# Block 1's activations fetched after the third modulation tile and built alternately with block 0's, in a four-branch decoder layer

## The chip, the cores and the metric

The kernel runs on one core of a Trainium2 chip. The metric is the device time of one execution in microseconds (us), the median of several runs; less is better. PE is the matrix engine, ACT the scalar engine, DVE the vector engine, POOL the GpSimd engine, and SP the queue from which most transfers are issued.

## The reference

One layer, 2048 tokens of width 1024. The conditioning vector gives a shift, a scale and a gate; the normalized input goes through one wide projection whose columns feed three branches (a gated linear recurrence, HGRN2 with 4 heads, a Mamba-2 scan with 16 heads); their outputs go through one output projection and a last normalization.

```python
cond = silu(c)
shift, scale, gate = split(cond @ w_ada + b_ada, 3)
h = rmsnorm(x, norm_w) * (1 + scale) + shift
u = h @ w_in                     # 1024 -> 5648 columns
a_x, a_g, hg_q, hg_f, hg_i, hg_g, ssd_z, ssd_xbc, ssd_dt = split(u)
ya = rg_lru(causal_conv(a_x)) * silu(a_g)
yb = rmsnorm(hgrn2(silu(hg_q), hg_f, hg_i)) * silu(hg_g)
yc = grouped_rmsnorm((ssd(xbc, dt) + d * xs) * silu(ssd_z))
out = rmsnorm(x + gate * (concat(ya, yb, yc) @ w_out), final_norm_w)
```

## The kernel before

The 2048 tokens are four blocks of 512 (tb 0 to 3), taken in two halves of two. Each block's normalized input is eight feature tiles of 128 x 512 (k = 0 to 7), stored as a rounded value and the rest (`ht`, two planes). Every projection is three matmuls per feature tile: high by high, high by low, low by high (`proj_mm`, L339). The weights are split the same way: ACT writes the rounded value, POOL or DVE the rest (`split`, L141 and L142).

**The order of instructions.** PE's order is the order of the code. On the other engines a scheduler chooses the order when the program is built; `after(ins, name)` adds an order without a wait on the chip. Each engine then works its list strictly in order. Loads of 256 KB go out from SP; each waits until the load eight places before it has landed.

**The start** is written out in the string `PROG`, one word per step, played by the loop over `PROG.split()`. `Xn` loads the eight feature tiles of block n (2 MB), `Dj` loads modulation tile j (four loads), `w0`/`w1` the two halves of the first head's three weights (three loads each), and `W0`/`W1` split them. `Sn` squares block n's tiles on ACT (`xsq`) and adds them on DVE, `Qn` sums over features on PE (`ps_ss`) and takes the root and reciprocal, and `Rn` spreads the result over the partitions on PE (`ps_rb`) and copies it out on ACT (`rb`). `Aj` multiplies modulation tile j on PE (`psm`, 8 instructions, 16 matmuls in the trace) and copies it out on ACT (`macc`); `Cj` turns it into a column on PE (`psm` again, 2 instructions) and DVE writes shift and scale for feature tile j (`gsc`). `Hnk` builds feature tile k of block n: DVE scales (`h_pre`, the `xt` row), ACT rounds (`ht`, L330), DVE writes the rest (`ht` again). `Mnk` multiplies it with all three weights: 9 matmuls, three each into `ps_f`, `ps_q` and `ps_g`. `Un` is n filler matmuls (`warm`), `B` starts the loading of later weights, `K` loads constants. `E` orders the first evacuations behind the last `H` step.

After the start come the two heads' value projections (`ps_v`) and the HGRN2 heads. `weave` lays the pieces of a generator such as `hgrn` between the pieces of the projections that run meanwhile, by weights: a branch's piece comes when its share of the total weight is reached. `hgrn` begins with small matmuls `ps_sA` that need `hg_q` and `hg_k`, and ends with `ps_o`, one PSUM bank from the pool `ps_oy`, which has a single bank.

For the second half, `norm_stats` squares and sums rows on ACT while the Mamba part runs (`xst`); `norm_gen` (L883), called in step i = 2 of the recurrence part for block 2 and at the head of the second half for block 3, takes root and reciprocal of `xst` and goes straight on to `ps_rb`:

```python
    def norm_gen(xs, st):
        rb = norm_rows(rsqrt_cols(st))
        yield
```

At the end the output projection runs in units of one token tile and one branch; `fetch` (L912) loads the branch's result for the next unit, rounds it on ACT and writes the rest (`yy`) on POOL.

Of the kernel before, what the change touches and what calls it, by code (L numbers as in the profile page):

```python
# [8 lines left out]
F32 = mybir.dt.float32  # L9
F32R = mybir.dt.float32r  # L10
BF16 = mybir.dt.bfloat16
U8 = mybir.dt.uint8
# [6 lines left out]
P = 128  # L19
# [12 lines left out]
for _name, _w in (("norm_w", 8), ("b_shift", 8), ("b_scale", 8), ("c", 8),  # L32
# [5 lines left out]
NCOL = _n  # L38
NTMP = 32
NW = 8  # L40
PROG = ("X0 D0 w0 D1 D2 S0 U8 A0 Q0 U1 C0 D3 R0 W0 A1 U1 C1 H00 D4 A2 M00 C2 H01 w1 W1 D5 A3 M01 C3 H02 D6 A4 M02 C4 H03 X1 "
        "A5 M03 C5 H04 D7 A6 M04 C6 H05 S1 M05 H06 Q1 A7 R1 M06 C7 H10 H07 B K M10 H11 M11 H12 M07 H13 M12 H14 M13 "
        "H15 M14 H16 M15 H17 E M16 M17")
LW = 4
BW = (4, 1)
L0 = 0.01
# [3 lines left out]
def trunk(ctx, tc, x, x_t, w_mod, w_gate, w_in, w_out, wa, wx, cols, rows, ident_in,  # L50
# [271 lines left out]
        act(rb, ps, AF.Copy)  # L322
        return rb

    def h_pre(xs, rb, k):
        stt(xs[k], xs[k], gsc[:, 1, k:k + 1], rb, MUL, MUL)

    def h_tile(xs, k, dep=None):
        ht = hp.tile([P, 2, TB], F32R, tag="h", name="ht")
        d_ = S.activation(ht[:, 0], xs[k], AF.Identity, bias=gsc[:, 0, k:k + 1])  # L330
        after(d_, dep)
        stt(ht[:, 1], xs[k], gsc[:, 0, k:k + 1], ht[:, 0], ADD, SUB)
        return ht, d_.ins.name

    PASSES = ((0, 0), (0, 1), (1, 0))

# [124 lines left out]
    def consts(dep):  # L461
        mf = tmp("mf", (P, 6, 32), bufs=1)
        for d_, s_ in ((mf, masks_in), (tri, tri_in)):
            after(nc.sync.dma_start(d_, s_), dep)
        for gi, wsrc in ((0, wa), (1, wx)):
            for hh in range(2):
                after(nc.sync.dma_start(wab[hh * 64:(hh + 1) * 64, gi, :, hh * 64:(hh + 1) * 64],
                                        wsrc.rearrange("(t two) i j -> two i t j", two=2)[hh]), dep)
        after(nc.sync.dma_start(rowp, rows[0:1, 0:32].to_broadcast([P, 32])), dep)
        V.tensor_copy(maskd, mf[:, 0])  # L470
        V.tensor_copy(masks, mf[:, 1:6])

    def early():
        e4 = tmp("e4", (P, 4), bufs=1)
        p4 = tmp("p4", (P, 4), bufs=1)
        cs4 = tmp("cs4", (P, 4), bufs=1)
        tt(V, e4, cc("hlb", 0, 4), cc("hlb", 0, 4), MAX)
        tt(V, e4, cc("hlb", 0, 4), e4, SUB)
        sact(e4, e4, AF.Exp)
        V.reciprocal(p4, e4)  # L480
        tt(V, p4, e4, p4, MUL)
        V.tensor_copy(cs4, p4)
        tt(V, omlb[:, 0], cs4, p4, SUB)
        V.tensor_scalar(omlb[:, 1], omlb[:, 0], -1.0, 1.0, op0=MUL, op1=ADD)
        V.tensor_scalar(e4, cc("lam", 0, 4), -1.0, None, op0=MUL)
        softplus(cpos[:, 1], e4, 4, sact)
        V.tensor_scalar(cpos[:, 1], cpos[:, 1], 8.0, None, op0=MUL)
        V.tensor_scalar(cpos[:, 0], cpos[:, 1], -1.0, None, op0=MUL)
        V.tensor_scalar(dhalf, cc("sd", 0, 8), 0.5, None, op0=MUL)

    early()
# [61 lines left out]
    def hgrn(h, tbs, fq, vs, acc, first):  # L553
# [85 lines left out]
        st = hst[h]  # L639
        for n, tb in enumerate(tbs):  # L640
            v, gs, f, pkv = vs[tb], GS[n], Fs[n], pkvs[n]
            po = bank(ps_oy, "oy", "ps_o", (P, 4, P))
            for c in range(4):
                ci = 4 * tb + c
                PE.matmul(po[:, c], v[:, c], ssb[:, 4 * n + c], start=True, stop=ci == 0)  # L645
                if ci == 0:
                    V.tensor_copy(st, pkv[:, c])
                else:
                    PE.matmul(po[:, c], st, Qs[n][:, c * P:(c + 1) * P], start=False, stop=True)
                    if ci < 4 * NTB - 1:  # L650
                        stt(st, st, Tm[n][:, c:c + 1], pkv[:, c], MUL, ADD)
                if c < 3:
                    yield
            pof = po.rearrange("p c n -> p (c n)")
            if not first:
                act(f, pof, AF.Square)
                tt(G, acc[tb], acc[tb], f, ADD)
            else:
                act(acc[tb], pof, AF.Square)
            tt(V, gs, pof, gs, MUL)  # L660
            put_y(tb, 4 + h, gs)
            yield
# [218 lines left out]
        yield  # L881

    def norm_gen(xs, st):  # L883
        rb = norm_rows(rsqrt_cols(st))
        yield
        for k in range(KT):
            h_pre(xs, rb, k)
            if k % 4 == 3:
                yield
# [2 lines left out]
        for w_ in itertools.islice(g, n):  # L892
            yield w_

    def gap():
        yield

    def h_build(tb, xs, hts, dep):
        for k in range(KT):
# [31 lines left out]
    for half in range(2):  # L931
# [4 lines left out]
        for p in range(2):  # L936
# [26 lines left out]
            if half == 0 and p == 0:  # L963
# [3 lines left out]
                             bank(ps_mm, "mm", "ps_g") if tb == 0 else bank(ps_oy, "oy", "ps_g")]  # L967
                        for tb in tbs}
                xsb, sts, u_, dn, hn = {}, {}, None, None, None
                sqs = [[hp.tile([P, 2, TB], F32, tag="h", name="xsq") for _ in range(4)] for _ in tbs]  # L970
                x0s = [wp.tile([P, 2, TB], F32, tag="w", name="xt") for _ in range(4)]
                for op_ in PROG.split():
                    o_, ar = op_[0], [int(c) for c in op_[1:] if c.isdigit()]
                    if o_ == "D":
                        mod_dma(ar[0])
                    elif o_ == "A":
                        mod_mm(ar[0])
                    elif o_ == "C":
                        mod_col(ar[0])
                    elif o_ == "X":  # L980
                        xsb[ar[0]] = load_x(ar[0], x0s if ar[0] == 0 else None)
                    elif o_ == "S":
                        sts[ar[0]], dn = norm_sum(xsb[ar[0]], sqs[ar[0]])
                    elif o_ == "Q":
                        sts[ar[0]] = norm_cols(sts[ar[0]])
                    elif o_ == "R":
                        sts[ar[0]] = norm_rows(sts[ar[0]])
                    elif o_ == "E":
                        evac[0] = hn
                    elif o_ == "H":  # L990
                        h_pre(xsb[ar[0]], sts[ar[0]], ar[1])
                        HTS[ar[0]][ar[1]], hn = h_tile(xsb[ar[0]], ar[1])
                    elif o_ == "w":
                        for b_ in WBL[0:3]:
                            if ar[0] == 0:
                                b_.alloc()
                            b_.fetch(ar[0])
                    elif o_ == "W":
                        for b_ in WBL[0:3]:
                            b_.parts(ar[0], *((dn, V) if ar[0] == 0 else (hn, G)))  # L1000
                    elif o_ == "U":
                        pu = bank(ps_ms, "ms", "warm", (P, 4, P))
                        for _ in range(ar[0]):
                            PE.matmul(pu, ones, ones.unsqueeze(1).to_broadcast([P, 4, P]), start=True, stop=True)
                    elif o_ == "K":
                        consts(u_)
                    elif o_ == "B":
                        blocks.dep = u_
                        blocks.pump()
                    elif o_ == "M":  # L1010
                        tb, k = ar
                        for w_, ps in zip((wf, wq, wg), accs[tb]):
                            u = u_ = proj_mm(ps, w_, HTS[tb][k], k)
# [20 lines left out]
                    run(ps_, pend)  # L1034
            if half == 1 or p == 1:
                first = []
            pend = [(hgrn(h, tbs, {tb: fq[h, tb] for tb in tbs}, {tb: vs[tb][0] for tb in tbs}, acc, h == 0), HGW)]
            h += 1
            ps_ = first
            for f in (pf, pq_, pg):  # L1040
# [1 line left out]
                for tb in tbs:  # L1042
                    ps_ += f(w, h, tb)
            run(ps_, pend)
            pend = [(hgrn(h, tbs, {tb: fq[h, tb] for tb in tbs}, {tb: vs[tb][1] for tb in tbs}, acc, False), HGW)]
        if half == 0:
            act(aneg, rowp[:, 16:32], AF.Exp)
            V.tensor_scalar(aneg, aneg, -1.0, None, op0=MUL)
        dt_ = [(ssd_dt(tb, dtr[tb], dts), 1) for tb in tbs]
        st_ = [(stats(acc[tb], 0, tb), 2) for tb in tbs]  # L1050
        pend = dt_ + pend + st_
# [31 lines left out]
        for i in range(4):  # L1083
# [5 lines left out]

            def pgl(tb):  # L1090
                return p_proj(wg, HTS[tb], "ps_lg", lambda ps: gs.__setitem__(tb, lru_g(ps)))
            if i == 2 and half == 0:
                xs_ = load_x(2)
                pend += [(norm_gen(xs_, xst[0]), 3)]
# [122 lines left out]

    for u in range(len(units)):
        if u + 1 < len(units):
            fetch(u + 1)  # L1220
        pcs = unit(u) if u + 1 < len(units) else last_unit(u)
        if u == 0:
            weave(pcs, pend)
            for k in (12, 13, 14, 15):
                OBlock(k, hp, "h", h_use[id(HTS[3][2 * (k - 12) + 1])])
            OBlock(0, op, "wo")
        elif u == 1:
            weave(pcs, [(gate_rows(), 1)])
            OBlock(1)
            OBlock(2)  # L1230
            OBlock(3)
        else:
            for f in pcs:
                f()
        if units[u][1] == FAMS[-1] and u + 1 < len(units):
            for t in groups[units[u][0]]:
                finish(t)
# [60 lines left out]
```

## Time and profile before

| | |
|---|---|
| median of 3 runs | 1697.59 us (1697.58 to 1697.99) |
| the profiled execution | 1699.3 us, of which span 1697.5 us |
| PE busy | 1653.0 us, 97% of the span |
| PE weight loads | 1349.2 us, 79% |
| DVE / ACT / POOL busy | 971.5 / 748.6 / 757.3 us (57%, 44%, 45%) |
| mean granted PE clock | 0.992 |
| DMA | 150.60 MB, mean 89 GB/s; 333 GB/s in the first fortieth of the span |

The span is one execution from its first to its last instruction. Busy shares are averages over stages; where PE is busy all the time, only work taken from PE or waits of PE shorten the run. A busy PE at a lower clock is still counted as busy. "Granted clock" is the share of full speed (2.4 GHz) that PE had; 0.50 is 1.2 GHz.

### The profile page before, as it was taken

To read this page: it belongs to the slowest core of one execution; us is meant where nothing else is said; L and a number is where in the kernel's file an instruction comes from. 1 tells how busy PE (TensorE), PEld (TensorE's weight loads), DVE (VectorE), ACT (ScalarE), POOL (GpSimd) and SP (SyncE) were. 2 spreads that over 40 slices of the span, in tenths; PEclk is the share of its full clock that TensorE was granted. 3 is DMA by queue.
4 is the path that set the end of the run, shared out by engine and by line. 5 is a ranking of instruction groups with operands and counts; after the bars stand their busy time and mean duration, and the time that the engine had idled before them with its cause. 6 is when DMAs were issued, how large, how long until landed. Compare 5 with 4: busy or idle time off the path is not lost.

```text
span 1697.5 us, 29336 instructions
## 1 busy us (share of the span) xinstructions
PE 1653.0 (97%) x11452; PEld 1349.2 (79%) x11452; DVE 971.5 (57%) x1726; ACT 748.6 (44%) x1640; POOL 757.3 (45%) x630
## 2 busy tenths in 40 slices
PE   8799999999999999899999999999999999999998
PEld 4688877888887877788887788888877777888886
DVE  5654766557645746646756555655568646444443
ACT  4422323366556656632322456554757623222221
POOL 1233344355635764345334346545756543222223
PEclk9899999999999999999999999999999999999999
DMA  9412010032425342231110032323334544333231
GB/s 333 116 26 63 27 39 26 26 113 82 116 71 155 88 125 76 62 89 45 29 55 27 27 100 75 94 56 106 88 103 133 171 120 150 97 96 99 89 93 61
DMA packets 177691, 150.60 MB, mean 89 GB/s; under 512 B 14545, under 2 KB 137937, under 8 KB 177553
## 3 DMA queue, kind: packets, MB, share of 16 engines
q1 hardware_dynamic: 141216, 123.82, 25.1%
q10 hardware_dynamic: 33936, 17.04, 3.4%
q0 software_dynamic: 2400, 7.87, 1.3%
q8 instruction: 90, 1.47, 0.4%
q14 instruction: 49, 0.39, 0.1%
HBM read 123.40 MB, written 25.30 MB: 88 GB/s over the span
## 4 chain that ended last, share of the span: by engine, by line
PE 85%; DVE 4%; DMA 3%; ACT 3%; issue 3%; POOL 2%; SPq 0%; POOLq 0%; ACTq 0%; DVEq 0%
PE po L1138 19%; PE ps_x L339 10%; PE ps_z L339 9%; PE ps_v L345 6%; PE ps_f L339 5%; PE ps_g L339 5%; PE ps_bc L339 5%; PE ps_q L339 4%; PE ps_lg L339 4%; PE ps_lx L339 4%; PE ps_y L792 2%; PE ps_bx L768 2%; PE ps_y L797 1%; PE ps_sA L565 1%; PE ps_o L645 1%
## 5 line engine op out<-in xcount | busy, mean ns | idle before, releaser
L1138 PE MATMUL po<-wo,yy 128*128 128x512 f32 x1512 | 353.3, 395 | 2.5 <-POOL yy L69 1.6
L1138 PEld LDWEIGHTS po<-wo,yy 128*128 128x128 f32 x1512 | 283.8, 188 | 71.5 <-POOL yy L69 2.4
L142 POOL TENSOR_TENSOR w<-raw,w 128x512 fp32r<-128x512 f32 x156 | 219.6, 1426 | 266.9 <-ACT w L141 223.4
L72 DVE SCALAR_TENSOR_TENSOR cacc<-craw,col,cacc 128x512 f32<-128x512 f32 x192 | 203.8, 1062 | 47.6 <-ACT cacc L66 36.3
L339 PE MATMUL ps_z<-ht,w 128*128 128x512 f32 x768 | 190.2, 399 | 0.8 <-ACT halo L66 0.8
L339 PE MATMUL ps_x<-ht,w 128*128 128x512 f32 x768 | 190.4, 400 | 0.0
L339 PEld LDWEIGHTS ps_z<-ht,w 128*128 128x128 f32 x768 | 141.9, 188 | 34.7 <-issue 2.1
L339 PEld LDWEIGHTS ps_x<-ht,w 128*128 128x128 f32 x768 | 141.1, 189 | 28.6
L72 DVE SCALAR_TENSOR_TENSOR o<-po,rstd,o 128x512 f32<-128x512 f32 x64 | 47.2, 749 | 119.4 <-PE po L1138 98.8
L69 POOL TENSOR_TENSOR yy<-yr,yy 128x512 fp32r<-128x512 f32 x61 | 78.7, 1310 | 80.7 <-ACT yy L66 73.4
L69 POOL TENSOR_TENSOR hg_k<-hg_k,hg_t 128x256 f32<-128x256 f32 x80 | 60.2, 770 | 120.6 <-PE ps_sA L565 61.3
L141 ACT ACTIVATE w<-raw 128x512 fp32r<-128x512 f32 x158 | 92.3, 627 | 42.0 <-issue 22.0
L339 PE MATMUL ps_f<-ht,w 128*128 128x512 f32 x384 | 99.5, 406 | 5.4 <-DVE ht L72 5.4
L339 PE MATMUL ps_bc<-ht,w 128*128 128x512 f32 x384 | 101.0, 406 | 0.0
L345 PE MATMUL ps_v<-vw,ht 128*128 128x264 f32 x768 | 98.8, 289 | 0.0
L339 PE MATMUL ps_q<-ht,w 128*128 128x512 f32 x384 | 98.7, 403 | 0.0
L339 PE MATMUL ps_lx<-ht,w 128*128 128x512 f32 x384 | 97.7, 408 | 0.0
L345 PEld LDWEIGHTS ps_v<-vw,ht 128*128 128x128 f32 x768 | 95.7, 191 | 1.2 <-DVE l_gs L69 0.2
L69 POOL TENSOR_TENSOR s_ce<-s_ce,cacc 128x512 f32<-128x512 f32 x64 | 93.5, 1481 | 1.5 <-ACT s_ce L66 1.5
L339 PE MATMUL ps_lg<-ht,w 128*128 128x512 f32 x384 | 93.2, 397 | 0.0
L339 PE MATMUL ps_g<-ht,w 128*128 128x512 f32 x336 | 92.0, 408 | 0.0
L339 PEld LDWEIGHTS ps_f<-ht,w 128*128 128x128 f32 x384 | 71.2, 191 | 23.4 <-DVE ht L72 5.7
(260 smaller groups left out, 2853.1 us busy)
## 6 DMA issues: line engine op xcount, KB each, us to landing
raw<-in_w_in SPq DMA_DIRECT2D x176, 256.0 KB, 3.2
s_cb<-crd SPq DMA_DIRECT2D x64, 256.0 KB, 3.8
yr<-yscr SPq DMA_DIRECT2D x64, 256.0 KB, 3.2
xr<-in_x SPq DMA_DIRECT2D x48, 256.0 KB, 3.4
xt<-in_x_t SPq DMA_DIRECT2D x32, 256.0 KB, 4.7
wta<-in_w_mod SPq DMA_DIRECT2D x32, 256.0 KB, 5.9
yscr<-cacc ACTq DMA_DIRECT2D x32, 256.0 KB, 2.7
rawo<-in_w_out SPq DMA_DIRECT2D x32, 256.0 KB, 3.9
```

Source lines behind the costliest of these rows:

```text
L69: e.tensor_tensor(o, a, b, op=op)
L72: V.scalar_tensor_tensor(o, a, s, b, op0=op0, op1=op1)
L141: after(S.activation(hi, raw, AF.Copy), None if eng is V else dep)
L142: after(eng.tensor_tensor(lo, raw, hi, op=SUB), dep if eng is V else None)
L339: d_ = PE.matmul(ps, b.hl[wl][:, k, :], ht[:, hl, :], start=(k == 0 and n == 0), stop=(k == KT - 1 and n == 2))
L345: d_ = PE.matmul(ps[:, 0:264], ht[:, hl, c * P:(c + 1) * P], b.vw[k // 4][wl][:, k % 4, :], start=(k == 0 and n == 0), stop=(k == KT - 1 a ...
L565: PE.matmul(out(n, c, r), Ks[n][:, o:o + 32], mv[n][..., o + sh:o + sh + 32], start=True, stop=True)
L645: PE.matmul(po[:, c], v[:, c], ssb[:, 4 * n + c], start=True, stop=ci == 0)
L768: PE.matmul(pkv[:, c].rearrange("p h n -> p (h n)"), bt[:, c], xw[:, c].rearrange("p h n -> p (h n)"), start=True, stop=True)
L792: PE.matmul(py[64 * hh:64 * hh + 64, c], xdt[:, c, hh], Ms[hh][:, c], start=True, stop=sv[tb][c] is None)
L797: PE.matmul(py[64 * hh:64 * hh + 64, c], sv[tb][c][:, 64 * hh:64 * hh + 64], Cs[hh][:, c * P:(c + 1) * P], start=False, stop=True)
L1138: PE.matmul(pss[t, n], yys[u, t][yl][:, k4, :], wts[4 * fam + k4][wl][n], start=(k4 == 0 and i == 0), stop=(k4 == 3 and i == 2))
```

## The change

`PROG` is rewritten. `X1` stands after `D2` (it stood after `H03`), and the steps of block 1 alternate with those of block 0, so that the eight `M` steps of block 1 no longer follow the block 0 steps. Two more filler matmuls (`U2`) stand ahead of `M03`. `h_pre` gets an order: behind the second-last feature tile's low part on DVE. The staging tiles change pools: block 0's x lies in the pool of the feature tiles, the squares of both blocks share four tiles in the weight pool. The row constants load from ACT's queue at the start. The root of `xst` for both blocks is taken in step i = 1. Every `hgrn` gets a `gap(2)` ahead of it, the second `ps_o` takes a bank of the pool `ps_sc`, and the rest `yy` for units 4 and 5 is written by DVE.

```diff
-PROG = ("X0 D0 w0 D1 D2 S0 U8 A0 Q0 U1 C0 D3 R0 W0 A1 U1 C1 H00 D4 A2 M00 C2 H01 w1 W1 D5 A3 M01 C3 H02 D6 A4 M02 C4 H03 X1 "
...
+PROG = ("X0 D0 w0 D1 D2 X1 S0 U8 A0 Q0 U1 C0 D3 R0 W0 A1 U1 C1 H00 H01 A2 M00 C2 w1 H02 M01 S1 M02 D4 A3 Q1 C3 R1 H03 "
...
-    def h_pre(xs, rb, k):
-        stt(xs[k], xs[k], gsc[:, 1, k:k + 1], rb, MUL, MUL)
+    def h_pre(xs, rb, k, dep=None):
+        after(V.scalar_tensor_tensor(xs[k], xs[k], gsc[:, 1, k:k + 1], rb, op0=MUL, op1=MUL), dep)
...
-        after(nc.sync.dma_start(rowp, rows[0:1, 0:32].to_broadcast([P, 32])), dep)
...
     def early():
+        nc.scalar.dma_start(rowp, rows[0:1, 0:32].to_broadcast([P, 32]))
...
+        sact(aneg, rowp[:, 16:32], AF.Exp)
+        V.tensor_scalar(aneg, aneg, -1.0, None, op0=MUL)
...
-            po = bank(ps_oy, "oy", "ps_o", (P, 4, P))
+            pool, tag = ((ps_oy, "oy"), (ps_sc, "sc"))[n]
+            po = bank(pool, tag, "ps_o", (P, 4, P))
...
     def norm_gen(xs, st):
-        rb = norm_rows(rsqrt_cols(st))
+        rb = norm_rows(st)
...
-    def gap():
-        yield
+    def gap(w=1):
+        yield w
...
-                sqs = [[hp.tile([P, 2, TB], F32, tag="h", name="xsq") for _ in range(4)] for _ in tbs]
-                x0s = [wp.tile([P, 2, TB], F32, tag="w", name="xt") for _ in range(4)]
+                x0s = [hp.tile([P, 2, TB], F32, tag="h", name="xt") for _ in range(4)]
+                sqs = [wp.tile([P, 2, TB], F32, tag="w", name="xsq") for _ in range(4)]
+                los = [None, None]
...
-                        h_pre(xsb[ar[0]], sts[ar[0]], ar[1])
-                        HTS[ar[0]][ar[1]], hn = h_tile(xsb[ar[0]], ar[1])
+                        h_pre(xsb[ar[0]], sts[ar[0]], ar[1], los[-2])
+                        HTS[ar[0]][ar[1]], hn, ln = h_tile(xsb[ar[0]], ar[1])
+                        los.append(ln)
...
-            pend = [(hgrn(h, tbs, {tb: fq[h, tb] for tb in tbs}, {tb: vs[tb][0] for tb in tbs}, acc, h == 0), HGW)]
+            pend = [(gap(2), 2), (hgrn(h, tbs, {tb: fq[h, tb] for tb in tbs}, {tb: vs[tb][0] for tb in tbs}, acc, h == 0), HGW)]
...
+            if i == 1 and half == 0:
+                xst = {n: rsqrt_cols(st) for n, st in xst.items()}
...
-            fetch(u + 1)
+            fetch(u + 1, V if u + 1 in (4, 5) else G)
```

The order on PE in the start, from step `C2` on. `ps_f`, `ps_q` and `ps_g` with three matmuls each are one `M` step; `psm` x2 is a `C` step and `psm` x8 an `A` step. Before:

```order
L450 MATMUL psm<-ones,macc 128x1 x2
L441 MATMUL psm<-wta,condz 32x256 x8
L339 MATMUL ps_f<-ht,w 128x512 x3
L339 MATMUL ps_q<-ht,w 128x512 x3
L339 MATMUL ps_g<-ht,wt 128x512 x3
```

And now, from `M02` on, which directly follows `M01`:

```order
L339 MATMUL ps_f<-ht,w 128x512 x3
L339 MATMUL ps_q<-ht,w 128x512 x3
L339 MATMUL ps_g<-ht,wt 128x512 x3
L441 MATMUL psm<-wta,condz 32x256 x8
L311 MATMUL ps_ss<-ones,xsq 128x1 x4
L450 MATMUL psm<-ones,macc 128x1 x2
L320 MATMUL ps_rb<-ident,xsc 128x128 x4
L1009 MATMUL warm<-ones 128x512 x2
```

Before, each step of block 0 has its `C`, `A` and `M` in turn, and block 1's sum (`ps_ss`) and spreading (`ps_rb`) stand after `M06`. Now `M02` is followed by `A3`, and the sum and the spreading stand ahead of `M03`, with two fillers.

The order on ACT around the second modulation tile's copy (`macc`). Before:

```order
L66 ACTIVATE rb<-ps_rb 128x512
L141 ACTIVATE wt<-raw 128x512
L330 ACTIVATE ht<-xt,gsc 128x512
L66 ACTIVATE macc<-psm 128x256
L330 ACTIVATE ht<-xt,gsc 128x512
```

And now:

```order
L66 ACTIVATE rb<-ps_rb 128x512
L141 ACTIVATE wt<-raw 128x512
L66 ACTIVATE xsq<-xt 128x512
L330 ACTIVATE ht<-xt,gsc 128x512
L66 ACTIVATE xsq<-xt 128x512
L66 ACTIVATE macc<-psm 128x256
L66 ACTIVATE xsq<-xt 128x512 x4
```

Two squares of block 1 now stand ahead of the second `macc`; each needs its tile of block 1's x from memory.

The order on ACT where the roots of `xst` are taken. Before, for block 3, at the head of the second half:

```order
L152 ACTIVATE l_i<-ps_i,col 128x512
L152 ACT_TABLE_LOAD
L152 ACTIVATE xst<-xst,epsc 128x4
L141 ACTIVATE w<-raw 128x512 x2
L66 ACTIVATE rb<-ps_rb 128x512
```

And now, for both blocks, in the recurrence part's first step:

```order
L152 ACTIVATE l_gs<-ps_lg 128x512
L152 ACT_TABLE_LOAD
L152 ACTIVATE xst<-xst,epsc 128x4 x2
L66 ACTIVATE s_z<-cacc 128x512
L520 DMA yscr_100<-cacc 128x4x128
L152 ACT_TABLE_LOAD
L152 ACTIVATE l_r<-ps_r,col 128x512
```

The root for block 3 stood just ahead of the copy `rb` that needs it; now both roots stand between two steps of the recurrence, with a table load on each side.

## Rows read from the trace of the kernel before

**Rows 1.** PE's waits over the span: total us, times, longest.

```profile
PE ps_rb L320 <- DVE xst L285: 7.3, 2, 5.5
PE ps_f L339 <- DVE ht L72: 5.4, 1, 5.4
PE ps_ss L311 <- DVE xsq L305: 3.9, 1, 3.9
PE psm L450 <- ACT macc L66: 2.9, 1, 2.9
...
PE ps_o L645 <- DVE hg_g L69: 1.9, 2, 1.1
...
PE po L1138 <- POOL yy L69: 1.6, 2, 0.9
```

**Rows 2.** Windows: length, busy PE, PEld, DVE, ACT, POOL (count), clock, DMA.

```profile
50.00:55.00 5.00, 3.81 (x25) 2.55 (x26) 1.41 (x5) 0.31 (x2) 0.00 (x0) 0.50 0.63 157
...
65.00:70.00 5.00, 5.00 (x12) 3.91 (x13) 4.84 (x7) 4.17 (x7) 2.58 (x2) 0.51 0.03 10
...
85.00:90.00 5.00, 3.18 (x77) 2.48 (x76) 4.73 (x8) 3.73 (x8) 2.96 (x3) 1.00 0.00 0
```

**Rows 3.** Timeline of PE in the start: start us, us, what [idle before].

```profile
14.65 1.05 PE L311 MATMUL ps_ss<-ones,xsq 128*128 128x1 f32 x8
15.57 1.10 PE L1004 MATMUL warm<-ones 128*128 128x512 f32 x2
16.51 0.50 PE L450 MATMUL psm<-ones,macc 128*128 128x1 f32 x4
16.87 1.14 PE L320 MATMUL ps_rb<-ident,xsc 128*128 128x128 f32 x8
...
38.80 0.96 PE L339 MATMUL ps_f<-ht,w 128*128 128x512 f32 x3
...
40.99 0.50 PE L450 MATMUL psm<-ones,macc 128*128 128x1 f32 x4
41.42 1.07 PE L441 MATMUL psm<-wta,condz 128*32 128x256 f32 x16
...
85.10 0.86 PE L339 MATMUL ps_g<-ht,wt 128*128 128x512 f32 x3
...
88.36 0.65 PE L565 MATMUL ps_sA<-hg_q,hg_k 128*32 128x64 f32 x32 [1.82 <-POOL hg_q L69]
88.95 6.07 PE L345 MATMUL ps_v<-vw,ht 128*128 128x264 f32 x48
```

**Rows 4.** The chain that ended last, first 130 us: start us, us, what.

```profile
13.06 5.69 DMA wta<-in_w_mod
...
18.77 5.86 DMA wta<-in_w_mod
```

**Rows 5.** Timeline of ACT, in the start and in the recurrence part.

```profile
42.65 0.38 ACT L66 ACTIVATE macc<-psm 128x256 f32<-128x256 f32 x1 [2.72 <-PE psm L441]
42.93 0.71 ACT L330 ACTIVATE ht<-xt,gsc 128x512 fp32r<-128x512 f32 x1
43.54 4.26 ACT L66 ACTIVATE xsq<-xt 128x512 f32<-128x512 f32 x8
...
607.99 1.28 ACT L152 ACT_TABLE_LOAD   x1
```

**Rows 6.** Timeline of DVE in the start.

```profile
46.91 0.75 DVE L72 SCALAR_TENSOR_TENSOR xt<-xt,gsc,rb 128x512 f32<-128x512 f32 x1
```

**Rows 7.** Timeline of POOL in the start.

```profile
67.42 3.43 POOL L142 TENSOR_TENSOR vw<-raw,vw 128x512 fp32r<-128x512 f32 x2 [4.56 <-DVE ht L72]
```

**Rows 8.** Timeline of PE where the second half's blocks are normalized.

```profile
647.65 1.16 PE L320 MATMUL ps_rb<-ident,xst 128*128 128x128 f32 x8 [1.79 <-DVE xst L285]
...
693.01 2.08 PE L320 MATMUL ps_rb<-ident,xst 128*128 128x128 f32 x8 [5.51 <-DVE xst L285]
694.74 5.47 PE L345 MATMUL ps_v<-vw,ht 128*128 128x264 f32 x31
```

More of the change, by code (lines that the diff above doesn't have):

```diff
@@ L40 @@
 NW = 8
-PROG = ("X0 D0 w0 D1 D2 S0 U8 A0 Q0 U1 C0 D3 R0 W0 A1 U1 C1 H00 D4 A2 M00 C2 H01 w1 W1 D5 A3 M01 C3 H02 D6 A4 M02 C4 H03 X1 "
-        "A5 M03 C5 H04 D7 A6 M04 C6 H05 S1 M05 H06 Q1 A7 R1 M06 C7 H10 H07 B K M10 H11 M11 H12 M07 H13 M12 H14 M13 "
-        "H15 M14 H16 M15 H17 E M16 M17")
+PROG = ("X0 D0 w0 D1 D2 X1 S0 U8 A0 Q0 U1 C0 D3 R0 W0 A1 U1 C1 H00 H01 A2 M00 C2 w1 H02 M01 S1 M02 D4 A3 Q1 C3 R1 H03 "
+        "H10 U2 W1 M03 D5 A4 M10 H11 C4 M11 H12 H04 M12 H13 M13 D6 A5 M04 H14 C5 H05 M14 D7 A6 M05 H15 C6 H06 M15 A7 M06 H16 C7 "
+        "H07 B K M16 H17 E M07 M17")
 LW = 4
@@ L331, in h_tile @@
         after(d_, dep)
-        stt(ht[:, 1], xs[k], gsc[:, 0, k:k + 1], ht[:, 0], ADD, SUB)
-        return ht, d_.ins.name
+        e_ = V.scalar_tensor_tensor(ht[:, 1], xs[k], gsc[:, 0, k:k + 1], ht[:, 0], op0=ADD, op1=SUB)
+        return ht, d_.ins.name, e_.ins.name
     PASSES = ((0, 0), (0, 1), (1, 0))
@@ L982, in trunk @@
                     elif o_ == "S":
-                        sts[ar[0]], dn = norm_sum(xsb[ar[0]], sqs[ar[0]])
+                        sts[ar[0]], dn = norm_sum(xsb[ar[0]], sqs)
                     elif o_ == "Q":
@@ L1044, in trunk @@
             run(ps_, pend)
[L1045 to L1048, printed above, removed]
+            pend = [(gap(2), 2), (hgrn(h, tbs, {tb: fq[h, tb] for tb in tbs}, {tb: vs[tb][1] for tb in tbs}, acc, False), HGW)]
         dt_ = [(ssd_dt(tb, dtr[tb], dts), 1) for tb in tbs]
```

## The prediction

> **What bounds the kernel now.** I read the page first: PE is busy 97% of the span, every other engine under 60%, so only PE's waits and PE's low clock are to be had. I then listed PE's waits [rows 1]. The reader is to see that few places hold nearly all the idle time: the spreading of the row norms in the middle (`ps_rb`, 7.3 us), three waits in the start (5.4 + 3.9 + 2.9 us), and small ones of 1 to 2 us. Next I asked for the granted clock in short windows [rows 2]: it is 0.50 and 0.51 in the two stretches behind the start's 3.9 and 5.4 us waits, and 1.00 in the stretch that holds the 1.82 us wait of [rows 3]. A long wait is thus paid twice: about 5 us at half clock is another 2.5 us of work, while a wait below 2 us costs itself alone. Last come the timelines of PE, ACT and DVE for the prices of single steps [rows 3, 5, 6].
>
> **The start, before.** The last `M` step ends at 85.10 + 0.86 = 85.96 us [rows 3]. Its waits have one cause: block 1's x is loaded late, its squares are summed late, and block 1's eight `M` steps, all at the end, wait for DVE.
>
> **The start, changed: when PE can go on.** Loads share one stream. The 18th load landed at 13.06 + 5.69 = 18.75 and the 26th at 18.77 + 5.86 = 24.63 [rows 4], so 0.735 us each. Block 1's x now takes places 24 to 31. Its first tile lands at 24.63 - 2 x 0.735 = 23.2. On ACT, two squares now stand ahead of the second `macc`, so this copy, which PE needs for `C1`, is held: 23.2 + 0.53 (square, 4.26 / 8) + 0.71 (`ht`) + 0.53 + 0.38 (`macc`) = 25.3 us [rows 5]. Before, ACT had nothing to wait for there. This is a new wait: behind it on PE stand `C1`, `A2` and everything else. PE has finished `A1` and a filler by about 21, so it idles some 4 us; by [rows 2] I charge 2.5 us of low clock behind it.
>
> The Trainium skill ("TensorE: Matmul & The Clock Gate", Part 1: The HAM clock gate) says that the array is throttled by default and that only recent activity releases it. The two slow stretches of [rows 2] agree.
>
> From 25.3 PE has this work, by start-to-start times where two rows stand next to each other, durations elsewhere [rows 3]: 16 `M` at 40.99 - 38.80 = 2.19 (35.0), 6 `A` at 1.07 (6.4), 7 `C` at 41.42 - 40.99 = 0.43 (3.0), the sum `ps_ss` 15.57 - 14.65 = 0.92, two fillers at 16.51 - 15.57 = 0.94 (1.9) and `ps_rb` 1.14. Together 48.4. Is PE kept fed? `M02` is not: behind `C2` its tile needs two of block 1's adds, its own scaling, ACT's rounding and DVE's rest, five steps of about 0.75 [rows 5, 6], 3.75 in all, while PE has only `M01`, 2.19: it waits 1.6. After that the fillers and `A4` give DVE its lead: a tile costs DVE 2 x 0.75 = 1.5, an `M` costs PE 2.19, so PE is the slower. Only `M07`, one step behind `C7`, may wait again: 0.5. The later modulation tiles need buffers that `M` and `A` steps release, but tile 7 is used about 15 us after that and is covered. Sum: 25.3 + 48.4 + 2.5 + 1.6 + 0.5 = 78.3, a gain of 7.7. Durations overlap a little and some `M` steps follow each other directly, so I take 8.1, bounds 3 (two more waits of the size of `M02`'s with one more slow stretch) and 12 (no slow stretch, no wait of `M02`).
>
> **Behind the start.** `ps_sA` waited 1.82 us for `hg_q`, which came 88.36 - 85.96 = 2.4 us after the last `M`. With the gap, 24 matmuls of `ps_v` at 6.07 / 48 = 0.126 us (3.0 us) stand ahead [rows 3]. But block 0's last `M` now ends only one step before block 1's, so its four evacuations (about 0.5 each) stand ahead of block 1's on ACT: 2.4 + 2.0 against 3.0 leaves 1.4 of wait. Gain 0.4; bounds 0 and 1.8.
>
> **The roots.** In [rows 8] PE waited 1.79 and 5.51 us for the reciprocal of `xst`. Behind the second wait `ps_rb` took 2.08 instead of 1.16, and 31 `ps_v` took 5.47 instead of 31 x 0.126 = 3.9. That is 1.79 + 5.51 + 0.92 + 1.57 = 9.8. The sums `xst` are complete well before the recurrence part, so early roots leave nothing to wait for. What is late next is the copy `rb` and block 3's tiles; [rows 1] has a single wait for `ht`, the start's, so there is room. In the new place ACT pays two table loads of 1.28 [rows 5] and two short roots, some 3 us, between two recurrence steps; PE runs projections meanwhile whose banks are free. If that cover were gone it would cost those 3 us. I take 9.5, bounds 5 and 9.8.
>
> **The small edits.** A second bank for `ps_o` ends its 1.9 us [rows 1]; the gap shifts the first step of every head by about two projection pieces and squeezes the following ones, which may give or cost some tenths at each head: I take 2.0 for both, bounds 0 and 4. Of the 1.6 us for `yy` the larger wait, 0.9, is before a unit whose `yy` DVE now writes; the other unit keeps POOL: 0.9, bounds -0.5 (DVE works its list in order, and a late load would block its evacuations) and 1.6. The constants on ACT's queue, the order hint and the exchanged pools cost nothing of their own: ACT waits for its first input anyway, the hint shapes the DVE order already counted, and the pools set only when buffers come free. If they were exposed, under 1 us.
>
> **Sum.** 8.1 + 0.4 + 9.5 + 2.0 + 0.9 = 20.9. The profiled execution, 1699.3 us with a span of 1697.5, would go to 1678.4; the median of the runs, 1697.6, stands 1.7 below the profiled one, and goes to 1676.7.
>
> **The rivals.**
> *The start gives nothing.* Every step of the start now hangs on in-order lists. ACT splits the value weights only behind the last `macc`, and POOL writes four rests at 3.43 / 2 = 1.7 us beside DVE [rows 7]: 6.9 us, against three `M` steps and a `C` before `ps_v`, 7.0. A little lateness makes PE wait there. For it: [rows 1] shows that such waits did decide the start. Against it: the weights' loads need no late buffer. Then the 8.5 us go and 1685 is left.
> *More than forecast.* No slow stretch, `M02` fed, `ps_sA` and the heads' waits gone: the upper bounds 12 + 1.8 + 9.8 + 4 + 1.6 = 29, time 1668.5.
> *Slower: PE stays at 1.2 GHz through the alternating steps.* The place is the stretch from `C1` on, whose matmuls wait briefly for tiles again and again. An `M` then costs about 2.2 more; all 16 cost 35, less the 2.5 already charged: 32.5 - 20.9 gives 1709. From about ten slow `M` steps on the change loses. For it: the new 4 us wait. Against it: in [rows 3] the same `C`, `A`, `M` alternation ran at 2.19, full speed. The rule of the skill cited above is what would bring this about.
> *The change does not do what it says:* the early x moves the start's waits to the modulation tiles behind it, whose loads come eight places later, and in the roots' place PE waits for `rb`. The time stays near 1697. Against it: eight places are 8 x 0.735 = 5.9 us, less than the start's waits together.
>
> **How the numbers follow.** Forecast 0.64, own range 1671 to 1682; nothing from the start 0.15; more 0.11; slower 0.07; no effect 0.03. The range 1668 to 1687 takes in the second and third case and leaves out 0.10. What differs by over 0.2%, 3.4 us, can be told from no change: faster 0.64 + 0.15 + 0.11 = 0.90, same 0.03, slower 0.07.
>
> **What would show it.** In the changed profile PE waits near 21 to 25 us for ACT's `macc`, the clock is low for about 5 us behind it, then PE is nearly gapless and the last `M` ends near 78. The two waits of `ps_rb` for `xst` are gone and the clock around the second stays at 1.00. The waits of `ps_o` for `hg_g` are gone, that of `ps_sA` is 1 to 2 us. The prediction is wrong if the last `M` ends after 83 or before 74, if `ps_v` waits for `vw`, or if PE waits for `rb` or `ht` where it waited for `xst`.

## The result, and the profile after

The changed kernel takes 1678.88 us (median of four runs, 1676.8 to 1679.21) beside 1697.79 us for the kernel before on the same chip, a ratio of 0.9879 (95% interval 0.9859 to 0.9899): 20.5 us less, between 17.1 and 23.9. The two medians are 18.9 us apart; the ratio is formed over all runs, and of the four before, one took 1702.84, the others 1697.58 to 1697.99. The prediction said 1676.7, with 1668 to 1687 as its range. The profiled execution has a span of 1676.9 us against 1697.5, 20.6 less. PE's busy time went from 1653.0 to 1648.6 us, 98% of the span: 4.4 us of the gain are busy time (slow stretches that went, less two more fillers), the rest is idle time of PE.

PE's waits in the changed kernel, where [rows 1] stood (total us, times, longest):

```profile
PE psm L450 <- ACT macc L66: 2.3, 1, 2.3
PE ps_f L339 <- DVE ht L332: 2.2, 4, 1.0
PE ps_f L339 <- ACT ht L330: 1.6, 3, 0.9
```

`ps_rb` and `ps_o` wait for neither `xst` nor `hg_g` any more. In the start the wait for `macc` is a new one, that of `C1`; the 2.9 us of [rows 1] were `C3`'s and are gone. There are also a number of small waits for `ht`. The timeline of PE there (start us, us, what, [idle before]) answers [rows 3]:

```profile
19.52 1.94 PE L441 MATMUL psm<-wta,condz 128*32 128x256 f32 x16
...
24.92 0.98 PE L450 MATMUL psm<-ones,macc 128*128 128x1 f32 x4 [2.33 <-ACT macc L66]
...
27.69 1.65 PE L339 MATMUL ps_f<-ht,w 128*128 128x512 f32 x3
...
31.70 0.56 PE L450 MATMUL psm<-ones,macc 128*128 128x1 f32 x4
...
35.39 0.50 PE L339 MATMUL ps_f<-ht,w 128*128 128x512 f32 x1 [0.94 <-ACT ht L330]
...
55.40 0.73 PE L339 MATMUL ps_f<-ht,w 128*128 128x512 f32 x2 [1.00 <-DVE ht L332]
...
79.34 0.73 PE L339 MATMUL ps_f<-ht,w 128*128 128x512 f32 x2 [0.66 <-DVE ht L332]
...
80.60 0.86 PE L339 MATMUL ps_g<-ht,wt 128*128 128x512 f32 x3
81.30 3.06 PE L345 MATMUL ps_v<-vw,ht 128*128 128x264 f32 x24
84.28 1.21 PE L567 MATMUL ps_sA<-hg_q,hg_k 128*32 128x64 f32 x64
85.43 6.07 PE L345 MATMUL ps_v<-vw,ht 128*128 128x264 f32 x48
```

`C1` starts at 24.92, `M00` takes from 27.69 to 31.70 (4.0 us, where 2.19 is full speed), and the last `M` ends at 81.46, 4.5 us ahead of the 85.96 of before. `ps_sA` no longer waits. After it, `ps_v` goes on at 85.43 with 24 matmuls done; before, it began at 88.95 with none [rows 3]. At equal work that is 88.95 + 3.0 - 85.43 = 6.5 us. Two windows of the start hold most of the time at the low clock (length, busy PE, granted clock, DMA share, GB/s):

```profile
15.00:20.00 5.00, 4.50 (x29) 0.82 1.08 375
...
25.00:30.00 5.00, 5.00 (x26) 0.50 1.07 374
```

The second is the stretch behind `C1`'s wait. The first is another one: from about 18.4 to 21.7 us the granted clock was 0.50, and `A1` took 1.94 us instead of 1.07, although PE had waited no more than 0.35 us at a time since 12.25. It cost nothing here, since `C1` waits for ACT afterwards: in the second run of the same kernel (`a0_again`) `A1` ran at full clock, and `C1` started at 25.25 after a wait of 3.72.

Further on, the same matmuls can be found in both traces. The timeline of PE after; `ps_rb` answers [rows 8]:

```profile
620.93 1.02 PE L832 MATMUL ps_r<-cacc,wab 128*128 128x512 f32 x2
...
675.77 1.06 PE L320 MATMUL ps_rb<-ident,xst 128*128 128x128 f32 x8
...
688.78 5.82 PE L339 MATMUL ps_f<-ht,w 128*128 128x512 f32 x24 [0.70 <-ACT dtr L66]
...
695.84 1.02 PE L832 MATMUL ps_r<-cacc,wab 128*128 128x512 f32 x2
...
936.08 0.49 PE L652 MATMUL ps_o<-hg_q,hst 128*128 128x128 f32 x2 [0.35 <-DVE hst L72]
```

and of before, the matmuls that correspond to `ps_r` and to the last of these, with one pair from a recurrence step that is used below:

```profile
148.43 1.62 PE L339 MATMUL ps_g<-ht,w 128*128 128x512 f32 x6
150.18 0.46 PE L645 MATMUL ps_o<-ssb,hg_v 128*128 128x128 f32 x2
...
630.47 1.02 PE L829 MATMUL ps_r<-cacc,wab 128*128 128x512 f32 x2
...
714.18 1.02 PE L829 MATMUL ps_r<-cacc,wab 128*128 128x512 f32 x2
...
956.42 0.49 PE L649 MATMUL ps_o<-hg_q,hst 128*128 128x128 f32 x2 [0.22 <-DVE hst L72]
```

The lead is 6.5 us behind the start, 630.47 - 620.93 = 9.5 ahead of the roots, 18.3 behind them, 20.3 at the last head and 20.6 at the end. Set against the terms of the sum:

| term | predicted | by these points | run alone (below) |
|---|---|---|---|
| start, to the last `M` | 8.1 | 4.5 | 4.6 (3.1 to 6.1), with a longer wait of `ps_sA` |
| `ps_sA` | 0.4 | 2.0 | in the gap |
| gap, second bank of `ps_o` | 2.0 | 3.0 + 2.0 = 5.0 | gap 1.2 (-0.3 to 2.6), bank 6.0 (3.9 to 7.8) |
| roots | 9.5 | 8.8 | 9.0 (7.0 to 10.9) |
| `yy` | 0.9 | 0.3, all that comes behind the last head | not told from nothing |
| sum | 20.9 | 20.6 | |

The total was right within 2.2 us, but two terms were wrong by three and more, in opposite directions: that the sum came out is in part luck. The start's 4.5 also depends on the trace that it is set against (last section).

### The profile page after: what moved, and what is told of

It reads as the page before. It is cut to its first block, busy times and chain, and to the rows that moved or that the text cites. A ratio compares the mean times of both kernels' runs of the same rounds, so it can differ in the third digit from the quotient of the medians.

```text
span 1676.9 us, 29345 instructions
## 1 busy us (share of the span) xinstructions
PE 1648.6 (98%) x11456; PEld 1346.0 (80%) x11456; DVE 966.0 (58%) x1728; ACT 747.0 (45%) x1639; POOL 754.6 (45%) x628
## 3 DMA queue, kind: packets, MB, share of 16 engines
q8 instruction: 90, 1.47, 0.4%
## 4 chain that ended last, share of the span: by engine, by line
PE 87%; DVE 3%; DMA 3%; ACT 3%; POOL 2%; issue 2%; SPq 0%; POOLq 0%; ACTq 0%; DVEq 0%
PE po L1142 20%; PE ps_x L339 10%; PE ps_z L339 9%; PE ps_f L339 5%; PE ps_g L339 5%; PE ps_v L345 5%; PE ps_q L339 5%; PE ps_bc L339 5%; PE ps_lx L339 4%; PE ps_lg L339 4%; PE ps_y L795 2%; PE ps_bx L771 2%; PE ps_y L800 1%; PE ps_sA L567 1%; PE ps_sB L567 1%
## 5 line engine op out<-in xcount | busy, mean ns | idle before, releaser
L141 ACT ACTIVATE w<-raw 128x512 fp32r<-128x512 f32 x158 | 93.2, 628 | 39.0 <-issue 17.1
```

The source lines that it names most:

```text
L141: after(S.activation(hi, raw, AF.Copy), None if eng is V else dep)
```

## Experiments

Each was timed beside the kernel before on the same chip, whose median there was 1701.01, 1700.35 and 1701.3 us in the three groups of four. Ratios to it are compared, and medians only within a group.

**The four parts alone, each put into the kernel before.**

```diff
# e1_roots
-        rb = norm_rows(rsqrt_cols(st))
+        rb = norm_rows(st)
...
+            if i == 1 and half == 0:
+                xst = {n: rsqrt_cols(st) for n, st in xst.items()}
# e2_start: the changed kernel with the roots, the gap, ps_o's bank and fetch as they were before
# e3_gap, at both places where pend is set
-    def gap():
-        yield
+    def gap(w=1):
+        yield w
...
-            pend = [(hgrn(h, ...), HGW)]
+            pend = [(gap(2), 2), (hgrn(h, ...), HGW)]
# e4_ps_o
-            po = bank(ps_oy, "oy", "ps_o", (P, 4, P))
+            pool, tag = ((ps_oy, "oy"), (ps_sc, "sc"))[n]
+            po = bank(pool, tag, "ps_o", (P, 4, P))
```

> The kernel before with the roots of the rows alone moved to the earlier step. Theory: the two waits of ps_rb go with the slow stretch behind the second, 9.8 us by their rows, less the 0.8 us that the changed kernel's trace still waits for ACT in that place: 9.0 us faster, about 1688.8, no wait of ps_rb. Rival 1: rb or the next block's tiles take the place of the roots, and PE waits there for 3 us or more: at most 5 us faster. Rival 2: the part needs the other edits (the DVE and POOL lists of the whole kernel shift): less than 3 us.

Measured: 1692.69 us, ratio 0.9947 (0.9936 to 0.9959), 9.0 us less. The theory holds. In its timeline of PE the spreading no longer waits, and what is late next is a copy of `dtr`, by 1.65 us, twice what the theory left for it:

```profile
687.26 1.05 PE L320 MATMUL ps_rb<-ident,xst 128*128 128x128 f32 x8
...
700.88 5.37 PE L339 MATMUL ps_f<-ht,w 128*128 128x512 f32 x22 [1.65 <-ACT dtr L66]
```

> The kernel before with the start alone changed (order of its steps, exchanged pools, the order hint, constants on ACT's queue); no gap, one bank of ps_o, roots where they were. Theory from the changed kernel's trace: its last M ends 4.5 us earlier than before, and without the gap ps_sA waits about as long as it did (1.8 us): 4.5 us faster, about 1693.2. Rival 1, the prediction's sum: 7.7 to 8.1 us. Rival 2: block 0's evacuations now crowd block 1's, ps_sA waits 4 us, and only 2 us are left.

Measured: 1696.66 us, 0.9973 (0.9964 to 0.9982), 4.6 us less. The theory's number holds, its reason only in part. The prediction's 7.7 to 8.1 for the last `M` is not reached: it ends at 81.09 here. (With the 2.0 that the prediction charged for crowded evacuations its sum for this run would be 6.1, which the time alone doesn't exclude.) Without the gap `ps_sA` waits twice in its timeline, longer than the theory said, and the `ps_v` behind it run slowly:

```profile
81.90 0.65 PE L567 MATMUL ps_sA<-hg_q,hg_k 128*32 128x64 f32 x32 [0.81 <-POOL hg_q L69]
84.44 0.65 PE L567 MATMUL ps_sA<-hg_q,hg_k 128*32 128x64 f32 x32 [1.88 <-POOL hg_q L69]
85.02 7.25 PE L345 MATMUL ps_v<-vw,ht 128*128 128x264 f32 x45
```

The granted clock from 85 to 90 us was 0.66, and these 45 `ps_v` took 7.25 us, where 6.07 x 45 / 48 = 5.7 is full speed. The new start makes the wait longer (2.7 against 1.8), as the prediction argued, but the second half of `ps_sA` can go 84.44 - 81.09 = 3.35 us after the last `M`, and with 3.0 us of `ps_v` ahead and its own first half (0.6) it starts no sooner: the gap covers all of it, and the slow stretch goes too.

> The kernel before with the gap of two steps at each head alone. Theory: 24 matmuls of ps_v (3.0 us) stand ahead of ps_sA and cover its 1.8 us; at the last heads of each half the first step's wait of 0.6 us goes too, and its squeezed followers wait about as much longer: 1.8 to 3 us faster. Rival: the squeeze costs more than the waits return, within 0.5 us of before.

Measured: 1700.47 us, 0.9993 (0.9985 to 1.0002), 1.2 us less; the interval doesn't tell the two answers apart. The trace does: the wait of `ps_sA` is gone, but `ps_o` now waits for its bank five times, 4.3 us in its list of waits, where it was 1.9 in two [rows 1]. The gap shifts the recurrence onto that bank. Other waits of the heads only move: `ps_kt` from 0.8 to 2.3 us, `ps_sC` from 2.3 to 0.5.

> The kernel before with the second bank for ps_o alone. Theory: the waits of ps_o for the bank (1.1 and 0.8 us at the last heads of the halves, six of 0.1) go: 2.0 to 2.5 us faster. Rival: the second bank is taken from ps_sA, ps_sB and ps_sC, which then wait for each other: no gain or slower by 1 us.

Measured: 1694.83 us, 0.9965 (0.9954 to 0.9977), 6.0 us less: more than both answers. Most of this is how a wait is priced. In its timeline `ps_o` follows six `ps_g` like this:

```profile
147.11 1.63 PE L339 MATMUL ps_g<-ht,w 128*128 128x512 f32 x6
148.58 0.38 PE L646 MATMUL ps_o<-ssb,hg_v 128*128 128x128 f32 x2
```

From `ps_g` to `ps_o` it is 1.47 us, before 150.18 - 148.43 = 1.75, and there `ps_o` itself takes 0.07 more: 0.35 us lost, with no wait shown at all. A list counts idle time from the modelled end of the matmul before, but the next could have started ahead of that end (here `ps_o` starts at 148.58, and the end is put at 147.11 + 1.63 = 148.74). Six such places and the two listed waits (1.1 and 0.8, each with 0.24 on top) make 6 x 0.35 + 1.9 + 0.48 = 4.5 us. The traces agree: this one is 5.7 us shorter than that of before, and 1.3 of them lie in the start, which the edit doesn't touch (the long `ps_v` begins at 87.63, before at 88.95). The interval of the 6.0 takes in 4.5.

**The changed kernel again, with edits that price its new waits.** In `a1_squares` block 1's squares are ordered behind the second `macc`:

```diff
+        macc_i[j] = S.activation(mas[j][:, 0:2 * P], psm[:, 0:2 * P], AF.Copy).ins.name
...
-            act(sq, xs[k], AF.Square)
+            after(S.activation(sq, xs[k], AF.Square), dep)
```

> The changed kernel once more, beside the three that follow. Theory: the four parts added up (9.0 + 4.5 + 1.2 + 6.0 = 20.7 by the ratios of the parts run alone) give 1.2% less than before, 0.988, and the edit of yy next to nothing. Rival: the parts help or hinder each other by more than 2 us, 0.986 or 0.990.

Measured: 1678.47 us, 0.9871 (0.9856 to 0.9886). The parts alone multiply to 0.988: they add up within 2 us.

> The changed kernel with block 1's squares ordered behind the second macc on ACT. Theory: the wait of C1 for macc (2.3 us) comes from the two squares and the tile that stand ahead of that copy and wait for x; C1 then starts near 22.3 instead of 24.9, and the slow stretch behind it, in which M00 costs about 4.9 instead of 2.6, goes too: 4 to 5 us faster than the changed kernel. Rival 1: only the wait goes, PE's low clock stays with it: 2.3 us. Rival 2: M00 and M01 wait for their tiles instead, whose scaling and rests hang on DVE: less than 1 us.

Measured: 1674.12 us, 0.985 (0.9835 to 0.9865), 4.4 us under the median of the changed kernel in the same group; the runs of the two don't overlap (1673.96 to 1677.14, and 1677.67 to 1679.24). The cause of the wait can be read from ACT's timeline in the changed kernel: two squares, the first held 2.10 us by x, stand ahead of the copy.

```profile
22.84 0.63 ACT L66 ACTIVATE xsq<-xt 128x512 f32<-128x512 f32 x1 [2.10 <-DMA xt<-in_x_t]
23.37 0.71 ACT L330 ACTIVATE ht<-xt,gsc 128x512 fp32r<-128x512 f32 x1
23.99 0.61 ACT L66 ACTIVATE xsq<-xt 128x512 f32<-128x512 f32 x1
24.51 0.36 ACT L66 ACTIVATE macc<-psm 128x256 f32<-128x256 f32 x1
```

With the order changed, PE's timeline has `C1` 2.9 us earlier, and new small waits in its place:

```profile
21.98 0.61 PE L450 MATMUL psm<-ones,macc 128*128 128x1 f32 x4 [0.34 <-ACT macc L444]
...
26.88 0.61 PE L450 MATMUL psm<-ones,macc 128*128 128x1 f32 x4 [1.00 <-ACT macc L444]
```

and its window shows the full clock behind them:

```profile
25.00:30.00 5.00, 3.08 (x14) 1.00 1.06 377
```

So theory and rival 2 both had a share: wait and slow stretch went (2.9 + 3.1 us), and about 2.5 us came back as waits for `macc` and `ht`, since five squares stand ahead of the third `macc`. The last `M` ends at 77.9, 3.5 us earlier.

In `a2_gap_first` the edit is `pend = [(gap(2), 2)] * (h == 0 and half == 0) + [...]`; `a4_both` has this and the squares' order, and copies the masks behind the last tile.

> The changed kernel with the gap kept at the first head alone. Theory: with the second bank of ps_o in place the gap at the later heads only moves waits (ps_sA and ps_sC 1.3 us less, ps_kt and block 2's first head 1.7 us more in each half at most): within 1 us of the changed kernel, rather faster. Rival: the gap is worth its 2 us of the sum at the later heads: 2 us slower.

Measured: 1677.69 us, 0.9867 (0.985 to 0.9883), 0.8 less and within what runs differ by. So the rival's 2 us are not there: the gap at the later heads can't be told from nothing.

> The changed kernel with block 1's squares behind the second macc, the gap at the first head alone, and the copies of the masks on DVE behind the last tile. Theory: 4 to 5 us from the squares, 0.5 from the gap, 0.6 from the wait of M17 for its tile: 5 to 6 us faster than the changed kernel. Rival: M07's tiles now wait elsewhere, and the gain is that of the squares alone or less.

Measured: 1675.39 us, 0.9853 (0.9838 to 0.9867): the rival, no more than the squares alone. `M17` no longer waits for its tile, but `ps_sA` waits 0.94 us instead. In this execution the sixth tile of x also came later than in `a1_squares`; ACT's square waited for it, and behind it stood block 0's tile:

```profile
27.93 0.63 ACT L303 ACTIVATE xsq<-xt 128x512 f32<-128x512 f32 x1 [1.22 <-DMA xt<-in_x_t]
```

PE waited 1.86 us for that tile, and the window behind it was slow again:

```profile
30.00:35.00 5.00, 4.91 (x14) 0.71 1.06 339
```

**Two terms taken back, and the order carried on.** `b1_no_bank` and `b2_yy_pool` are the changed kernel with the bank, or the choice of engine in `fetch`, as before. `b3_order` has the gap at the first head alone and hangs the squares on block 0's tiles; `b4_order_w1` is `b3_order` with

```diff
-                            b_.parts(ar[0], *((dn, V) if ar[0] == 0 else (hn, G)))
+                            b_.parts(ar[0], *((dn, V) if ar[0] == 0 else (hn, V)))
```

> The changed kernel with ps_o back in one bank. Theory: the gap pushes the recurrence steps onto the bank; in the run with the gap alone ps_o waited eight times, 0.13 + 0.11 + 0.81 + 1.09 + 0.80 + 0.11 + 0.81 + 0.81 = 4.7 us, so 4.7 us slower than the changed kernel (1678.5). Rival, the sum on record: bank and gap together are worth 2.0, so 2 us slower at most.

Measured: 1685.6 us, 0.9908 (0.9895 to 0.9922), against 0.9871: 6.3 us slower than the changed kernel. The rival, the prediction's own figure, falls; the theory was too low for the reason found above. PE's timeline in it,

```profile
262.37 0.95 PE L339 MATMUL ps_g<-ht,w 128*128 128x512 f32 x3
264.12 0.46 PE L647 MATMUL ps_o<-ssb,hg_v 128*128 128x128 f32 x2 [0.80 <-DVE hg_g L69]
```

and in the changed kernel's second run:

```profile
262.71 0.94 PE L339 MATMUL ps_g<-ht,w 128*128 128x512 f32 x3
263.49 0.38 PE L648 MATMUL ps_o<-ssb,hg_v 128*128 128x128 f32 x2
```

1.75 from one to the next against 0.78, and 0.07 in `ps_o` itself: the listed 0.80 costs 1.04. By this count the five listed waits (4.3) and three that are not listed come to 4.3 + 5 x 0.24 + 3 x 0.35 = 6.6.

> The changed kernel with all rests of yy on POOL again. Theory from the changed kernel's trace: po waited 0.63 + 0.63 for yy, before 0.62 + 0.94, so 0.3 us slower. Rival, the sum on record: 0.9 us slower.

Measured: 1679.73 us, 0.9873 (0.9859 to 0.9886) against 0.9871: the time can't tell 0, 0.3 and 0.9 apart. A wait of 0.93 us for POOL's `yy`, which the changed kernel doesn't have, is back in its trace, so the edit does take the larger wait away. But the waits of `ps_r` and `po` from 1300 us on differ by 1 to 2 us in total among versions that don't touch that part (2.4 us in `a0_again`, 1.5 in `a2_gap_first`, 3.5 in `b4_order_w1`), so an edit of this size is lost among them.

> The changed kernel with the gap at the first head alone and block 1's squares ordered behind block 0's tiles: the first five behind the second tile on ACT, the last three behind the third. Theory: C1 starts near 22 at full clock, C2 no longer waits 1.0 us for macc behind squares, M01's and M02's waits (0.5 + 0.4, 0.8 + 0.3) shrink to about 1 us together: last M near 76.5, some 6 us faster than the changed kernel and 1.5 us faster than the version with the squares behind macc alone. Rival: block 1's sum of squares comes late instead, and PE waits for ps_ss or its tiles: no faster than that version (1674.1).

Measured: 1672.27 us, 0.9833 (0.982 to 0.9847), 1.7% under the kernel before and 0.4% under the changed one: the fastest of all, as the theory said. In its timeline of PE `C1` waits 0.25 us, `C2` and `M01` not at all, `M02` still 1.08 us for its tile, and the last `M` ends at 75.1, 6.4 us before that of the changed kernel:

```profile
21.50 0.61 PE L450 MATMUL psm<-ones,macc 128*128 128x1 f32 x4 [0.25 <-ACT macc L66]
...
74.22 0.86 PE L339 MATMUL ps_g<-ht,wt 128*128 128x512 f32 x3
```

> The same with the three rests of the first projection weights' second half on DVE instead of POOL. Theory: POOL's three rests (1.5 to 1.7 us each) slow the DVE steps that run beside them: a scaling takes 1.78 and two rests 3.47 instead of 0.75 each, 3.0 us more, and so a tile of block 1 is 1.15 us late. On DVE the three cost 2.1 us and nothing is slowed: the wait shrinks to 0 to 0.4, 0.8 to 1.1 us faster than the version before it. Rival 1: the 2.1 us stand in DVE's list at the wrong place, and the wait grows by 1 us. Rival 2: the DVE steps are as long without POOL's: the cause is another.

Measured: 1672.86 us, 0.9834 (0.9821 to 0.9848), no faster; the intervals are too wide to tell 1 us. The trace confirms the cause all the same. DVE's timeline in `b3_order`, with POOL's rests beside it,

```profile
39.22 1.78 DVE L326 SCALAR_TENSOR_TENSOR xt<-xt,gsc,rb 128x512 f32<-128x512 f32 x1
40.92 3.48 DVE L332 SCALAR_TENSOR_TENSOR ht<-xt,gsc,ht 128x512 fp32r<-128x512 f32 x2
```

and the same steps here, with POOL idle:

```profile
41.12 0.75 DVE L326 SCALAR_TENSOR_TENSOR xt<-xt,gsc,rb 128x512 f32<-128x512 f32 x1
41.78 1.63 DVE L332 SCALAR_TENSOR_TENSOR ht<-xt,gsc,ht 128x512 fp32r<-128x512 f32 x2
```

The wait of 1.0 us is gone, and at the last head PE is 1.4 us ahead of `b3_order`; the waits of `ps_r` and `po` at 1300 to 1360 us then take 1.7 us more. Whether these follow from loads or from the order of the lists there wasn't tried.

## Why the prediction was right, and where it wasn't

**The new wait of `C1` was right in place and size.** Forecast at 25.3, measured at 24.92, by the squares ahead of `macc`; the slow stretch behind it took 24.92 to 31.70, 6.8 us for 3.7 us of work: 3.1 against the 2.5 charged. `a1_squares` shows that both hang on that order. The idle time itself was 2.3 us, not "some 4", since `A1` ran slowly ahead of it.

**"Its waits have one cause" was too simple.** Of the waits in the start of before, `C3`'s had another. ACT rounds the second half of the first head's weights (`W1`, three steps) ahead of the copy that `C3` needs, and these steps wait for the weights' loads. The last of the three, and `C3`:

```profile
31.13 0.63 ACT L141 ACTIVATE wt<-raw 128x512 fp32r<-128x512 f32 x1 [0.21 <-DMA raw<-in_w_in]
```

```profile
32.09 0.79 PE L450 MATMUL psm<-ones,macc 128*128 128x1 f32 x4 [2.94 <-ACT macc L66]
```

It is the same pattern as the new wait of `C1`. In the new `PROG`, `W1` stands behind `U2`, and `C3` doesn't wait. The forecast did not need this, because it was added up from the work behind `C1`.

**The step of the start that failed is "a tile costs DVE 1.5, an `M` costs PE 2.19, so PE is the slower".** From `C1` to the last `M` PE took 56.5 us, not 53.0. By start-to-start times `M02` cost 1.8 (1.6 forecast) and `M07` 1.4 (0.5), but `M13` lost 1.7 and `M17` 0.9, which the sum had at nothing. DVE's timeline in the changed kernel, at `M13`, `M07` and `M17`:

```profile
45.59 1.78 DVE L326 SCALAR_TENSOR_TENSOR xt<-xt,gsc,rb 128x512 f32<-128x512 f32 x1
47.30 3.47 DVE L332 SCALAR_TENSOR_TENSOR ht<-xt,gsc,ht 128x512 fp32r<-128x512 f32 x2
...
73.01 0.86 DVE L69 TENSOR_TENSOR gsc<-gsc,col 128x1 f32<-128x1 f32 x1
...
77.50 1.78 DVE L332 SCALAR_TENSOR_TENSOR ht<-xt,gsc,ht 128x512 fp32r<-128x512 f32 x1
```

and POOL's at the same time:

```profile
45.49 3.04 POOL L142 TENSOR_TENSOR w<-raw,w 128x512 fp32r<-128x512 f32 x2 [42.55 <-ACT w L141]
48.48 1.74 POOL L142 TENSOR_TENSOR wt<-raw,wt 128x512 fp32r<-128x512 f32 x1
```

In these rows a step of 0.75 beside POOL takes 1.7 to 1.8. The 0.86 of `gsc`, ahead of `M07`'s tile, is 0.16 at the tiles before it; POOL wrote rests of the value weights at that time (71.32 to 73.85, and again 76.07 to 78.74). `b4_order_w1` shows the cause for `M13`: with POOL idle there the wait is gone. The Trainium skill ("SBUF — State Buffer", section "SBUF: two separate sides") says that a DVE operation with two SBUF inputs and a GpSimd operation hold the shared port pair in turn, each for its whole length. The rows agree in the main: each of the four steps takes 1.0 us more than alone. But strict turns would take more than was measured: three of DVE's alone are 2.25 us and three of POOL's, in the kernel before, 3.74, together 6.0, and from 45.49 to 50.77 all six took 5.3. In `a4_both` one rest on DVE took 0.79 (at 74.73) while POOL was at work, and POOL's two steps then took 3.03 instead of 2.53. That it is the port no run shows by itself. At `M17` the copies of the masks stood ahead of the tile as well; `a4_both` shows that without them `ps_sA` waits instead.

**`ps_sA`** was put at 1.4 us of remaining wait, and has none: the 3.0 us of `ps_v` cover even the longer wait that `e2_start` shows. There the second half came 3.35 us after the last `M`, 0.95 later than before; the sum had charged 2.0 for the crowded evacuations. That gave 1.6 us more than forecast.

**"A second bank for `ps_o` ends its 1.9 us" failed by size.** The mechanism is right, but the 1.9 us were two listed waits out of eight, each priced by its idle time alone. Counted from start to start it is 4.5 us, and `e4_ps_o` and `b1_no_bank` give 6.0 and 6.3, above the bound of 4 for gap and bank together. This and `ps_sA` made up for what the start lacked, which was luck: nothing in the sum tied the one to the other.

**The roots were right**: 8.8 by the traces and 9.0 alone, against 9.5. The clock at the second `ps_rb` stayed at full speed (1.06 us for eight, was 2.08). What was late next was not `rb`, as argued, but the copy of `dtr`, at 0.7 us (1.65 in `e1_roots`).

**The rivals.** The value weights were never waited for, so "the start gives nothing" did not happen. "More than forecast" asked for a start without a slow stretch and with `M02` fed; in `b3_order` the slow stretch is gone, `M02` still waits 1.08 us, and the time is 1672.3, not 1668.5. The modulation tiles that were loaded later were not waited for either: the only such wait, 2.4 us, is for the first one. PE did not stay at 1.2 GHz through the alternating steps: from `C1` on only `C1`, `A2` and the first `M` were slow, and the waits of up to 1.1 us between tiles left the clock at 1.00. The Trainium skill ("TensorE: Matmul & The Clock Gate", Part 1: The HAM clock gate) has the throttled clock as the default, which activity releases. The stretch behind `C1`'s wait agrees; the one at 18.4 to 21.7 us, ahead of which PE waited no more than 0.35 us at a time, is not explained by it.

**"A wait below 2 us costs itself alone" was read from one wait, and doesn't hold.** The 1.86 us in `a4_both` and the 1.88 us in `e2_start` were each followed by matmuls at 0.50; the latter cost 1.5 us more.

## What to carry to other kernels

Price a wait from the start of the matmul before to the start of the one that waited, and compare with the same pair where nothing waits: on the bank of `ps_o` the list left out 0.24 us of each wait that it had and six small ones altogether, and 1.9 us in the list were worth 4.5 by the trace and 6.0 by the time. When work is moved forward on an in-order engine, look at what stands behind its first instruction that waits for a load: two squares ahead of a copy cost 4 us, and an order hint that puts them behind the tiles brought the last `M` 6.4 us forward. And before counting an engine as the faster one, look at what runs on the other engines in that stretch, not at its step's time elsewhere.

## What was not expected of the hardware

Waits of the same length left different clocks. Behind the wait of `C1` (2.3 us, in `a0_again` 3.7) the granted clock was 0.50 in the next window, and behind the 1.86 us in `a4_both` it was 0.50 for some two microseconds (0.71 over five). But it was 1.00 behind the 1.82 us of [rows 3] [rows 2], behind `C3`'s waits of 2.5 us in `e3_gap` and 2.2 us in `e4_ps_o`, and behind the 2.84 us that `a0_again` waited for the first modulation tile at 12.55. And it fell to 0.50 at 18.4 us in the changed kernel without such a wait. The wait alone doesn't decide it, and what else does wasn't tried.

The start of before also varies by itself: with the same instructions up to there, the last `M` ended at 85.96 us in the kernel before, at 87.65 in `e1_roots`, 83.74 in `e3_gap` and 84.64 in `e4_ps_o`. `C3` waited 2.9, 3.5, 2.5 and 2.2 us in these, and the clock fell behind it in the first two alone. Set against these the changed kernel's 81.46 is 2.3 to 6.2 us earlier, so the 4.5 in the table is one draw. Single runs of the kernel before went from 1698.11 to 1703.7 us in the first group; the start's 4 us are a good part of that, and more than several of the edits that were to be measured.
